# A two-layer decoder kernel: the row-statistics matmuls of the attention contract over 128 rows, 64 of them zeros, instead of 64

## The chip, the core and the metric

The kernel runs on one core of one Trainium2 chip. The metric is device time in microseconds (us), the median of a few runs. The engines named below are TensorE (PE, with its weight loads shown as PEld), VectorE (DVE), ScalarE (ACT), GpSimd (POOL) and the queue of SyncE (SP), which issues most of the transfers (DMA).

## What is computed

Two consecutive layers of a decoder run for a prompt of 1024 tokens and for 32 sample tokens. The change lies in layer 0, in the attention of the prompt: one sliding-window attention A (8 query heads, 2 key heads, head dimension 64) and three dilated groups B of the same shape. The part of the reference that matters:

```python
def banded_attention(q, k, v, span, sink=None):
    # each block of 128 queries reads its own and the previous block of keys
    ...
    s = jnp.einsum('nbqhgd,nbkhd->nbhgqk', qb, kk, preferred_element_type=F32)
    ...
    p, den, lse = _softmax_stats(s, mask, sink_b)
    o = jnp.einsum('nbhgqk,nbkhd->nbqhgd', p, vv.astype(F32))

def _softmax_stats(s, mask, sink):
    s = jnp.where(mask, s, NEG_INF)
    m = s.max(-1)
    if sink is not None:
        m = jnp.maximum(m, sink)
    p = jnp.exp(s - m[..., None])
    den = p.sum(-1)
```

Layer 0 ends with an output projection and a layer norm; layer 1 is a chunkwise mLSTM that begins where layer 0 has ended.

## The kernel before

Operands of the matmuls are kept as a high and a low part (float32r), so that a projection is three matmuls for each 128 rows of the contraction: lines 199 to 201 in `proj_feat`, with 384, 384 and 288 tokens to a chunk. Layer 0 has 2016 of these, the keys' included ("projections" below).

The softmax's maximum of a row is taken ahead, from approximate scores. `stats` multiplies the high parts of the queries (`Qh`, 64 rows of head dimension, loaded by `qh_load`) with the high parts of the keys (rows 0 to 63 of `K1`), one matmul of 256 columns for each head and block of 128 queries (line 437): 256 of them, 8 for each of 32 loaded tiles `Qh`. DVE adds the mask and takes the maximum (line 441). A transpose (line 449) turns the maxima of one key head into rows; they go to DRAM, for B through a minimum over the three groups (`attn_b_max`, lines 564 and 568), and come back as row 65 of the tile `Q2`. Only then do the scores proper run in `scores`: lines 466 and 467 (128 rows of `K1` and `Q1`, then the 65 rows of `K2` and `Q2`) and, for the weighted values, lines 489 to 491. A block of scores is these two and three matmuls; attention A has 30 blocks and B has 70. The tiles `Q1` (512 KB) and `Q2` (260 KB) are loaded once for every two blocks of queries, 24 pairs for B.

`Qh` takes the buffers of `Q1` and `Q2` in turn, so that four of its tiles can be in flight; the scores use the same buffers. All these loads stand in one queue, SP's, in a fixed order with the weight loads (`wr`), and each waits there until its buffer is free.

Streams of work are emitted by `weave` in proportion to their work on PE. The statistics and scores have a priority ahead of the projections, so that the latter fill what the former leave. First the query projections are woven with attention A and with the statistics of groups 1 and 2, then the gate path (`proj_z0`) with the statistics of group 3 and with the scores of B. What is left of B's scores runs with the attention of the sample tokens and the merging of the heads. The order in which the instructions then stand on each engine is fixed when the program is built, and each engine takes its own in that order.

```python
Q1 = self.qh_load(0, kv, hf, ("Q1", "Q2")[hf % 2])
nc.tensor.matmul(st[:, u, :], Q1[:, h, q0:q0 + 128], K1[0:64, w0:w0 + 256], start=True, stop=True)
```

Of the kernel before, what the change touches and what calls it, by code (L numbers as in the profile page):

```python
# [26 lines left out]
def weave(*streams):  # L27
    """emit from several streams in proportion to their work on the tensor engine.
    A stream is (generator, total work); it yields the work that it emitted, or None to let the others go first."""
    live = [[g, 0.0, tot] for g, tot in streams]  # L30
    while live:
        for x in sorted(live, key=lambda x: x[1] / x[2]):
            try:
                w = next(x[0])
            except StopIteration:
                live.remove(x)
                break
            if w is not None:
                x[1] += w
                break  # L40


def ahead(tc, gen, offset):
    """the instructions of a stream, with a priority over what was emitted up to offset instructions before"""
# [14 lines left out]
# PSUM tags that the statistics, and the scores and outputs of the two halves of B, take in turn  # L59
STATS_PS = ("st", "sc")  # L60
AB_PS = ((("sc",), ("av",)), (("sc", "st"), ("av", "tr")), (("sc",), ("av", "pj", "pj")))
# by how many instructions the attention streams go ahead of what is woven with them
AHEAD = (1000, 1000, 60, 300)
# work of woven streams
W1, W2, W3, W4 = (129, 76), (86, 80), (28, 15, 6), (64, 90)
# steps of the second half of B that go with the gate path
EARLY = 9
# every how many blocks of B GpSimd takes the low parts
POOL_LO = 4
# tiles of tokens in the order of the output projections; the sample tokens are tile 8  # L70
ORDER = (0, 1, 2, 3, 4, 5, 6, 8, 7)
# stores on the queue of ScalarE, which makes the data
# [3 lines left out]
class Scratch:  # L76
    """cuts tiles that live together out of two large ones"""
# [20 lines left out]
class Builder:  # L98
# [20 lines left out]
    def wlo(self, out, in_, hi):  # L119
        """as lo, by GpSimd in layer 0"""  # L120
        if not self.layer:
            self.nc.gpsimd.tensor_tensor(out, in_, f(hi), OP.subtract)  # L122
        else:
            self.lo(out, in_, hi)

    def split(self, out, in_, scale=1.0):
        """high and low parts, out[:, 0] and out[:, 1]"""
# [3 lines left out]
    def products(self, ps, x, y, start, stop):  # L131
        """ps (+)= x.T y of operands in high and low parts"""
# [16 lines left out]
    def pair(self, pool, x):  # L149
        """[high | low] parts of the 32 sample tokens side by side"""  # L150
# [5 lines left out]
    def proj_tok(self, ps, i, X, xs, w):  # L156
        """token-major: ps[tokens of tile i, 512 features]; w(k) gives high and low parts of the weights.
        For the sample tokens (i = 8) the products with the low parts of x land in rows 32..63."""
# [13 lines left out]
    def samples(self, xs, x):  # L172
        """the sample tokens of the last chunk in one part"""
# [3 lines left out]
    def proj_sample(self, ps, k, xs, w):  # L177
        """part k of the contraction for the sample tokens, in full float32; four parts take the columns of the
        array side by side, and their products are left in 32 rows each"""
# [4 lines left out]
    def fold(self, out, ps):  # L184
        """the sum of the four parts of the sample tokens' products"""
# [4 lines left out]
    def proj_feat(self, src, X, evac, W=None, chunks=(0, 1, 2)):  # L190
        """feature-major: out[128 features, tokens]; yields after each chunk"""
# [165 lines left out]
    def qh_load(self, g, kv, hf, tag):  # L357
        """high parts"""
        Q = self.qp.tile([64, 4, 256], F32R, tag=tag, name="Qh")
        t = slice(256 * hf, 256 * hf + 256)  # L360
        h = slice(4 * kv, 4 * kv + 4)
        self.store("Qh", f(Q), self.QQ[g].rearrange("(d h) t -> d h t", h=8)[64:128, h, t])
# [37 lines left out]
    def v_load(self, g, kv):  # L400
        """[low | high | 1 1] of each block of keys"""
# [17 lines left out]
    def blocks(self, g, qb):  # L419
        """key blocks of query block qb: (block, kind); kind 0 own, 1 previous"""  # L420
# [3 lines left out]
    def stats(self, g, kv, hf, Q1, K1, ST):  # L424
        nc = self.nc
        for qb in range(2 * hf, 2 * hf + 2):
# [5 lines left out]
            for hp in range(2):  # L432
                st = self.pp.tile([128, 2, 256], F32, tag=STATS_PS[hp], name="st")
                for u in range(2):
                    h = 2 * hp + u
                    q0 = 128 * (qb % 2)
                    nc.tensor.matmul(st[:, u, :], Q1[:, h, q0:q0 + 128], K1[0:64, w0:w0 + 256], start=True, stop=True)  # L437
                for u in range(2):
                    h = 2 * hp + u
                    junk = self.sm.tile([128, 256], F32, tag="junk", name="junk", bufs=3)  # L440
# [4 lines left out]
    def neg_rows(self, ST, dst):  # L445
        """-max, rounded to float32r, as rows (h, qb) of 128 queries, to DRAM"""
# [48 lines left out]
    def od_view(self, OD, g, qb):  # L495
        """places in natural token order of query block qb"""
# [12 lines left out]
    def finish(self, ty, kv, sink_nm=None):  # L509
        """1/denominator rows to DRAM"""  # L510
# [3 lines left out]
        if sink_nm is not None:  # L514
            nm = self.sm.tile([32, 128], F32, tag="nmc", name="nmc")
            self.store('m', nm, sink_nm.rearrange("h (b q) -> (h b) q", q=128))
            e = self.sm.tile([32, 128], F32, tag="snk", name="snk")
            nc.scalar.activation(e, nm, AF.Exp, bias=self.sinkc[:, kv:kv + 1])
            nc.vector.tensor_tensor(dn, dn, e, OP.add)
        rc = self.sm.tile([32, 128], F32, tag="rc", name="rc")  # L520
        nc.vector.reciprocal(rc, dn)
        self.store('m', self.FD[ty][kv].rearrange("h (b q) -> (h b) q", q=128), rc)

    def attn_a(self, kv):
# [3 lines left out]
        for hf in range(4):  # L528
            Q1 = self.qh_load(0, kv, hf, ("Q1", "Q2")[hf % 2])
# [16 lines left out]
    def attn_b_stats(self, g, kv):  # L546
        K1 = self.k1_load(g, kv)
        ST = self.sm.tile([128, 32], F32, tag="ST", name="ST")
        for hf in range(4):
            Q1 = self.qh_load(g, kv, hf, ("Q1", "Q2")[hf % 2])  # L550
# [21 lines left out]
    def attn_b(self, kv, done=None):  # L572
        """the groups into one accumulator; done(c) is called when the tokens of chunk c are complete"""
# [26 lines left out]
    def proj_z0(self, j):  # L600
        nc = self.nc
        sz = self.stage.tile([128, T], F32, tag="sh", name="sz")
        if j < 4:
            kv, c = j // 2, 2 * (j % 2)
            o = self.tmp.tile([128, TP], F32, tag="ao", name="ao")
            F = self.tmp.tile([128, TP], F32, tag="aF", name="aF")
            for u in range(2):
                pr = slice(64 * u, 64 * u + 64)
                self.store('a', o[pr], self.OD[0][kv][0:64, c + u])
                self.store('a', F[pr], self.FD[0][kv][c + u].partition_broadcast(64))  # L610
            nc.gpsimd.tensor_tensor(o, o, F, OP.mult)
# [13 lines left out]
    # Scores have rows (sequence of a half, head, token) and one column per key. The 32 (head, token) queries of  # L625
    # a sequence are stationary, four sequences side by side in the array; the keys of the sequence move.
    def sample_queries(self, sp):
        """queries [128 (kv, d), seq, head, token] of each group, and masked scores of the new keys"""
# [34 lines left out]
    def sample_keys(self, src, g, a, st):  # L663
        """keys or values of the four sequences of half a, as [128, residues, 128] per sequence"""
        out = []
# [11 lines left out]
    def sample_group(self, g, st):  # L677
        """masked scores of the cached keys, and the maximum"""
# [27 lines left out]
    def sample_av(self, g, o, sp, st, first, last):  # L706
        """o[(seq, head, token), half, (kv, d)] += p^T v"""
# [29 lines left out]
    def sample_out(self, o, rec, ty, sp):  # L737
        """normalise, transpose, and place by (head parity, d), head pair, token"""
# [50 lines left out]
    def layer_norm(self, m, r, g, b):  # L789
        """LN(r) * g + b over 1024, in place; all in halves of 512"""  # L790
# [14 lines left out]
    def rstd(self, m, mv, eps, tag, scale=1.0):  # L805
        """(var scale + eps)^-0.5, with a Newton step after the first yield"""
# [12 lines left out]
    def merge0(self, ty, kv, c, M, inverse=True):  # L819
        """normalised attention outputs of four heads times the gate path, tokens of chunk c;  # L820
        the gate path of A has its prompt's outputs in it"""
# [67 lines left out]
    def layer0(self):  # L889
# [3 lines left out]
        # rows (part, d, head): low parts of 64 d, high parts of 64 d, -maximum  # L893
        self.QQ = [dt(f"QQ{g}", [129 * 8, TP]) for g in range(4)]
        self.QS = dt("QS", [4, 512, TS])
        # rows (part, d, head): high parts twice, low parts
        self.KK, self.KS = dt("KK", [3 * 512, TP]), dt("KSd", [512, TS])
        # per (group, kv head): low and high parts of 64 d
        self.VV = dt("VV", [TP, 8 * 128])
        self.NMB = [[dt(f"NMB{i}{g}", [4, TP]) for g in range(3)] for i in range(2)]  # L900
        # numerators of 64 d, denominator
# [12 lines left out]
        with tc.tile_pool(name="qp", bufs=2) as self.qp, tc.tile_pool(name="kp", bufs=2) as self.kp, \  # L914
# [8 lines left out]
            self.load(self.sinkc, A['sinkc'])  # L923
            run(self.proj_q(0))
# [97 lines left out]
    def gates(self):  # L1022
        """per-token gate quantities, in rows [4 heads, tokens]"""
# [596 lines left out]
```

## Time and profile before

| | |
|---|---|
| time, median of 3 runs | 1501.39 us (1501.26 to 1509.19) |
| span of the profiled execution | 1501.1 us |
| PE busy, share of the span | 1429.2 us, 95% |
| DVE busy | 882.7 us, 59% |
| statistics matmuls on PE (line 437) | 256, first at 169.2, last at 463.4 us |
| last projection of layer 0 | about 538 us |
| scores of B end | about 642 us |

The profiled execution's own time is not listed apart from its span; the span lies 0.3 us under the median. Busy time counts an instruction from its first to its last moment. Neighbouring matmuls overlap, so the price of one in a stream is the distance from its start to the start of the next.

### The profile page before, as it was taken

What the parts mean: (1) busy time and instruction counts of PE and PEld (TensorE: products, weight loads), DVE (VectorE), ACT (ScalarE), POOL (GpSimd) and SP (SyncE); (2) the same over time, 40 slices, a digit from 0 to 9 for tenths busy, and PEclk for the clock granted to TensorE, in tenths of its full rate; (3) what the DMA queues carried; (4) which work ended last, traced back from release to release, by engine and by line L of the source; (5) the groups of instructions that cost most, each with busy time, mean ns of one, the idle gap of its engine ahead of it and who ended that gap; (6) DMA issues with size and microseconds to landing.
All of it is one profiled execution on the core that took longest, in us unless ns stands there. A gap on an engine that the chain in (4) does not pass through costs nothing.

```text
span 1501.1 us, 21918 instructions
## 1 busy us (share of the span) xinstructions
PE 1429.2 (95%) x7792; PEld 1186.7 (79%) x7792; DVE 882.7 (59%) x2479; ACT 471.6 (31%) x892; POOL 264.6 (18%) x345
## 2 busy tenths in 40 slices
PE   8999999999999887889999999999999999998997
PEld 8989897977787754457878878988898899877785
DVE  5411455657665676778765536655565566566786
ACT  5331143431112464532123313331333133333310
POOL 1002242422233476501100000100000000000010
PEclk9999999999999997999999999999999999999999
DMA  8646455655766689995412665364323312341731
GB/s 306 224 147 215 161 176 179 206 177 178 198 175 180 187 216 234 273 291 167 156 51 72 202 223 200 96 199 132 77 78 117 117 50 68 116 131 23 249 132 46
DMA packets 148683, 241.01 MB, mean 161 GB/s; under 512 B 17504, under 2 KB 115776, under 8 KB 148056
## 3 DMA queue, kind: packets, MB, share of 16 engines
q1 hardware_dynamic: 140510, 218.24, 48.0%
q10 hardware_dynamic: 8064, 21.37, 4.0%
q8 instruction: 62, 1.02, 0.3%
q14 instruction: 47, 0.39, 0.1%
HBM read 178.66 MB, written 83.97 MB: 175 GB/s over the span
## 4 chain that ended last, share of the span: by engine, by line
PE 47%; DMA 9%; DVE 4%; issue 2%; ACT 1%; SPq 1%; POOL 0%; DVEq 0%; ACTq 0%; POOLq 0%
PE pj L199 5%; PE pj L201 5%; PE pj L200 5%; PE py L165 3%; PE py L167 3%; PE py L166 3%; PE pvo L165 3%; PE pvo L166 3%; PE pvo L167 3%; DMA Q<-QQ 3%; DMA G<-GR 2%; DMA out_cmems_dram<-Cs 1%; DMA wr<-in_wo_dram 1%; DMA mo<-OD 1%; PE S L1232 1%
## 5 line engine op out<-in xcount | busy, mean ns | idle before, releaser
L199 PE MATMUL pj<-xh,wh 128*128 128x384 f32 (+1 forms) x576 | 191.6, 333 | 0.2 <-DVE rt L214 0.2
L199 PE MATMUL pj<-x1h,wh 128*128 128x384 f32 (+1 forms) x576 | 189.6, 329 | 1.7 <-ACT QT L1153 1.6
L201 PE MATMUL pj<-xh,wl 128*128 128x384 f32 (+1 forms) x576 | 190.1, 330 | 0.0
L200 PE MATMUL pj<-xl,wh 128*128 128x384 f32 (+1 forms) x576 | 189.9, 330 | 0.0
L201 PE MATMUL pj<-x1h,wl 128*128 128x384 f32 (+1 forms) x576 | 187.7, 326 | 0.0
L200 PE MATMUL pj<-x1l,wh 128*128 128x384 f32 (+1 forms) x576 | 187.4, 325 | 0.0
L199 PEld LDWEIGHTS pj<-xh,wh 128*128 128x128 f32 x576 | 109.0, 189 | 9.4 <-ACT vv L112 0.8
L201 PEld LDWEIGHTS pj<-xh,wl 128*128 128x128 f32 x576 | 109.2, 190 | 6.0 <-issue 0.2
L200 PEld LDWEIGHTS pj<-xl,wh 128*128 128x128 f32 x576 | 109.2, 190 | 6.0
L199 PEld LDWEIGHTS pj<-x1h,wh 128*128 128x128 f32 x576 | 108.6, 189 | 6.5 <-issue 3.3
L201 PEld LDWEIGHTS pj<-x1h,wl 128*128 128x128 f32 x576 | 108.5, 188 | 6.0 <-issue 5.8
L200 PEld LDWEIGHTS pj<-x1l,wh 128*128 128x128 f32 x576 | 108.6, 189 | 4.0 <-issue 3.8
L441 DVE CUSTOM_DVE_ANT_0 junk<-st,maskq 128x256 f32<-128x256 f32 (+1 forms) x256 | 80.1, 360 | 43.4 <-PE st L437 32.5
L165 PE MATMUL pvo<-voh,x1h 128*128 128x512 f32 x256 | 101.0, 397 | 2.4 <-DVE SZ L1169 2.4
L166 PE MATMUL pvo<-voh,x1l 128*128 128x512 f32 x256 | 100.3, 394 | 0.0
L167 PE MATMUL pvo<-vol,x1h 128*128 128x512 f32 x256 | 99.6, 392 | 0.0
L811 POOL TENSOR_TENSOR rsw<-rsw,mhalf 128x1 f32<-128x1 f32 (+1 forms) x54 | 39.8, 738 | 323.5 <-DVE rsw L810 299.6
L122 POOL TENSOR_TENSOR wl<-wr,wh 128x1024 fp32r<-128x1024 f32 x24 | 57.3, 2389 | 152.4 <-ACT qs L233 102.9
L112 ACT ACTIVATE wh<-wr 128x1024 fp32r<-128x1024 f32 x48 | 50.7, 1056 | 94.5 <-PE pj L200 91.0
L116 DVE TENSOR_TENSOR pl<-p,ph 128x512 fp32r<-128x512 f32 x82 | 66.9, 822 | 21.6 <-ACT ph L112 19.6
L469 ACT ACTIVATE p<-sc 128x512 f32<-128x512 f32 x100 | 57.2, 593 | 59.1 <-PE sc L467 30.8
L112 ACT ACTIVATE ph<-p 128x512 fp32r<-128x512 f32 x100 | 60.7, 627 | 37.0 <-PE av L490 24.8
(348 smaller groups left out, 3109.6 us busy)
## 6 DMA issues: line engine op xcount, KB each, us to landing
Q<-QQ SPq DMA_DIRECT2D x32, 512.0 KB
out_kvs_dram<-in_cache_b_kv_dram SPq DMA_DIRECT2D x16, 1022.0 KB
wr<-in_w0f_dram SPq DMA_DIRECT2D x24, 512.0 KB
wr<-in_w1f_dram SPq DMA_DIRECT2D x24, 512.0 KB
Q<-QQ SPq DMA_DIRECT2D x32, 260.0 KB
QQ<-sh ACTq DMA_DIRECT2D x16, 512.0 KB
QQ<-sl ACTq DMA_DIRECT2D x16, 512.0 KB
Qh<-QQ SPq DMA_DIRECT2D x32, 256.0 KB
```

Of the source, the lines that this page charges most:

```text
L112: return self.nc.scalar.activation(out, in_, AF.Copy, scale=scale)
L116: return self.nc.vector.tensor_tensor(out, in_, f(hi), OP.subtract)
L122: self.nc.gpsimd.tensor_tensor(out, in_, f(hi), OP.subtract)
L165: nc.tensor.matmul(ps, xh[:, k, t], wh, start=k == 0, stop=False)
L166: nc.tensor.matmul(ps, xl[:, k, t], wh, start=False, stop=False)
L167: nc.tensor.matmul(ps, xh[:, k, t], wl, start=False, stop=k == 7)
L199: nc.tensor.matmul(ps[:, :n], wh[:, k, :], xh[:, k, :n], start=k == 0, stop=False)
L200: nc.tensor.matmul(ps[:, :n], wh[:, k, :], xl[:, k, :n], start=False, stop=False)
L201: nc.tensor.matmul(ps[:, :n], wl[:, k, :], xh[:, k, :n], start=False, stop=k == 7)
L441: nc.vector.tensor_tensor_reduce(junk[:, :n], st[:, u, c0:c0 + n], mk, 1.0, -3e38, OP.add, OP.max, ST[:, 8 * h + qb:8 * h + qb + 1])
L469: nc.scalar.activation(p, sc, AF.Exp)
L811: nc.gpsimd.tensor_tensor(r, v, self.mhalf[:m], OP.pow)
```

## The change

`stats` multiplies all 128 rows of `K1` (its rows 64 to 127 repeat the high parts) with a query tile of 128 rows whose rows 64 to 127 are zeros. The zeros are written once, so the query tiles can no longer be buffers that other tiles use: two tiles `QZ` live through the phase and take the loads in turn. Room for them comes from smaller scratch: one buffer `junk` for three, `finish` works in place, and the factor `F` of the gate path is loaded and applied in two halves of 512 tokens. Comments are dropped as well, which the diff here leaves out.

```diff
-    def qh_load(self, g, kv, hf, tag):
-        Q = self.qp.tile([64, 4, 256], F32R, tag=tag, name="Qh")
+    def qh_load(self, g, kv, hf):
+        Q = self.QZ[hf % 2]
         t = slice(256 * hf, 256 * hf + 256)
         h = slice(4 * kv, 4 * kv + 4)
-        self.store("Qh", f(Q), self.QQ[g].rearrange("(d h) t -> d h t", h=8)[64:128, h, t])
+        self.store("Qh", f(Q[0:64]), self.QQ[g].rearrange("(d h) t -> d h t", h=8)[64:128, h, t])
         return Q
...
-                    nc.tensor.matmul(st[:, u, :], Q1[:, h, q0:q0 + 128], K1[0:64, w0:w0 + 256], start=True, stop=True)
+                    nc.tensor.matmul(st[:, u, :], Q1[:, h, q0:q0 + 128], K1[:, w0:w0 + 256], start=True, stop=True)
...
-                    junk = self.sm.tile([128, 256], F32, tag="junk", name="junk", bufs=3)
+                    junk = self.sm.tile([128, 256], F32, tag="junk", name="junk", bufs=1)
...
-            e = self.sm.tile([32, 128], F32, tag="snk", name="snk")
-            nc.scalar.activation(e, nm, AF.Exp, bias=self.sinkc[:, kv:kv + 1])
-            nc.vector.tensor_tensor(dn, dn, e, OP.add)
-        rc = self.sm.tile([32, 128], F32, tag="rc", name="rc")
-        nc.vector.reciprocal(rc, dn)
-        self.store('m', self.FD[ty][kv].rearrange("h (b q) -> (h b) q", q=128), rc)
+            nc.scalar.activation(nm, nm, AF.Exp, bias=self.sinkc[:, kv:kv + 1])
+            nc.vector.tensor_tensor(dn, dn, nm, OP.add)
+        nc.vector.reciprocal(dn, dn)
+        self.store('m', self.FD[ty][kv].rearrange("h (b q) -> (h b) q", q=128), dn)
...
-            Q1 = self.qh_load(0, kv, hf, ("Q1", "Q2")[hf % 2])
+            Q1 = self.qh_load(0, kv, hf)
...
-            F = self.tmp.tile([128, TP], F32, tag="aF", name="aF")
             for u in range(2):
                 pr = slice(64 * u, 64 * u + 64)
                 self.store('a', o[pr], self.OD[0][kv][0:64, c + u])
-                self.store('a', F[pr], self.FD[0][kv][c + u].partition_broadcast(64))
-            nc.gpsimd.tensor_tensor(o, o, F, OP.mult)
+            for t in (slice(0, 512), slice(512, 1024)):
+                F = self.tmp.tile([128, 512], F32, tag="aF", name="aF")
+                for u in range(2):
+                    self.store('a', F[64 * u:64 * u + 64], self.FD[0][kv][c + u, t].partition_broadcast(64))
+                nc.gpsimd.tensor_tensor(o[:, t], o[:, t], F, OP.mult)
...
+            self.QZ = [sm.tile([128, 4, 256], F32R, name=f"QZ{u}") for u in range(2)]
+            for Q in self.QZ:
+                nc.gpsimd.memset(f(Q[64:128]), 0.0)
```

The order of the instructions changes with it. On PE, before, this is where the last statistics matmuls stand (`st`), among projections (`pj`) and ahead of the first scores (`sc`) of group 3; 201 of the 2016 projections stand behind them:

```order
L437 MATMUL st<-K_4017,Qh 128x256 x2
L199 MATMUL pj<-xh_100,wh 128x384
L437 MATMUL st<-K_4017,Qh 128x256 x2
L200 MATMUL pj<-xl_101,wh 128x384
L201 MATMUL pj<-xh_100,wl 128x384
L437 MATMUL st<-K_4017,Qh 128x256 x4
L199 MATMUL pj<-xh_100,wh 128x384
```

They stand close together there, the last four in a row. On PE in the changed kernel the same place, the last statistics matmuls and the first scores, reads:

```order
L437 MATMUL st<-K_3993,QZ_955 128x256 x2
L201 MATMUL pj<-xh_102,wl 128x384
L199 MATMUL pj<-xh_102,wh 128x384
L200 MATMUL pj<-xl_103,wh 128x384
L201 MATMUL pj<-xh_102,wl 128x384
L199 MATMUL pj<-xh_102,wh 128x384
L437 MATMUL st<-K_3993,QZ_955 128x256 x2
L200 MATMUL pj<-xl_103,wh 128x384
L201 MATMUL pj<-xh_102,wl 128x384
L199 MATMUL pj<-xh_104,wh 128x288
L466 MATMUL sc<-Q_4172,K_4159 128x512
L467 MATMUL sc<-Q_4174,K_4163 128x512
```

The statistics now end later among the projections: 98 of 2016 stand behind the last of them. Up to the last projection, 28 matmuls of lines 466 and 467 and 54 of lines 489 to 491 fewer have run than before; they stand behind it.

In SP's queue, before, this is a stretch of the gate path and of the statistics of group 2 (`Qh` from `QQ2`; `aF` and `ao` belong to `proj_z0`, `kt` holds keys, `wr` weights):

```order
L109 DMA Qh_3368<-QQ2_77 64x4x256
L109 DMA Qh_3398<-QQ2_77 64x4x256
L109 DMA aF_4294<-FD00_93 64x1024 x2
L109 DMA ao_4293<-OD00_89 64x1024
L109 DMA Qh_3455<-QQ2_77 64x4x256
L106 DMA kt_4018<-KK_80 128x1024
L109 DMA ao_4293<-OD00_89 64x1024
L109 DMA wr_5068<-in_w0f_dram 128x1024
```

Each `Qh` there is a tile of its own. In SP's queue in the changed kernel, the same stretch:

```order
L109 DMA aF_3818<-FD00_93 64x512 x2
L109 DMA QZ1_955<-QQ2_77 64x4x256
L109 DMA wr_5052<-in_w0f_dram 128x1024
L109 DMA aF_4268<-FD00_93 64x512 x2
L109 DMA ao_4265<-OD00_89 64x1024
L109 DMA QZ0_954<-QQ2_77 64x4x256
L109 DMA ao_4265<-OD00_89 64x1024
L109 DMA QZ1_955<-QQ2_77 64x4x256
L106 DMA kt_3994<-KK_80 128x1024
```

Two tiles alternate where each load had a buffer of its own among four, and the loads of `aF` are twice as many, half as large.

## Rows read from the trace of the kernel before

**Rows 1.** The page's busy times: engine, us (share of span), instructions.
```profile
PE 1429.2 (95%) x7792; PEld 1186.7 (79%) x7792; DVE 882.7 (59%) x2479; ACT 471.6 (31%) x892; POOL 264.6 (18%) x345
```
**Rows 2.** Windows: stretch, length, busy times; last three: clock, DMA share, GB/s.
```profile
160.00:463.40 303.40, 301.82 (x1610) 251.29 (x1609) 181.31 (x647) 83.44 (x148) 89.54 (x64) 0.99 0.61 183
463.40:538.50 75.10, 66.47 (x333) 54.38 (x332) 45.75 (x67) 33.59 (x62) 35.95 (x54) 0.98 0.67 182
538.50:642.00 103.50, 82.69 (x332) 42.21 (x331) 71.88 (x127) 56.95 (x106) 65.05 (x79) 0.85 0.95 252
```
**Rows 3.** Timeline of PE around groups of two and four: start, length, instruction.
```profile
391.19 0.34 PE L199 MATMUL pj<-xh,wh 128*128 128x384 f32 x1
391.37 0.33 PE L200 MATMUL pj<-xl,wh 128*128 128x384 f32 x1
391.63 0.73 PE L437 MATMUL st<-K,Qh 64*128 64x256 f32 x4
...
392.58 0.33 PE L199 MATMUL pj<-xh,wh 128*128 128x384 f32 x1
...
412.52 0.33 PE L200 MATMUL pj<-xl,wh 128*128 128x384 f32 x1
412.69 0.34 PE L201 MATMUL pj<-xh,wl 128*128 128x384 f32 x1
412.96 0.50 PE L437 MATMUL st<-K,Qh 64*128 64x256 f32 x2
413.39 0.44 PE L199 MATMUL pj<-xh,wh 128*128 128x384 f32 x1
413.67 0.34 PE L200 MATMUL pj<-xl,wh 128*128 128x384 f32 x1
```
**Rows 4.** Timeline of PE around two blocks of scores.
```profile
285.76 0.29 PE L201 MATMUL pj<-xh,wl 128*128 128x288 f32 x1
285.89 0.40 PE L466 MATMUL sc<-Q,K 128*128 128x512 f32 x1
286.13 0.39 PE L467 MATMUL sc<-Q,K 65*128 65x512 f32 x1
286.36 0.30 PE L199 MATMUL pj<-xh,wh 128*128 128x288 f32 x1
286.49 0.39 PE L466 MATMUL sc<-Q,K 128*128 128x512 f32 x1
```
**Rows 5.** Groups by line and shape, 160 to 480 us: busy, mean ns, idle before.
```profile
L201 PEld LDWEIGHTS pj<-xh,wl 128*128 128x128 f32 x420 | 79.3, 189 | 5.3 <-issue 0.2
L437 PEld LDWEIGHTS st<-K,Qh 64*128 64x128 f32 x256 | 36.8, 185 | 26.7 <-issue 15.0 <-DVE ST L441 7.3 <-DMA Qh<-QQ 2.0
```
**Rows 6.** Transfers from 538.5 to 642 us, all queues.
```profile
DMA packets 21235, 26.10 MB, mean 252 GB/s; under 512 B 1952, under 2 KB 18602, under 8 KB 21227
```
**Rows 7.** Timelines: loads of Qh, their use, and the pair before one.
```profile
226.84 1.33 SPq L109 DMA_DIRECT2D Qh<-QQ  x2
...
232.19 0.53 PEld L437 LDWEIGHTS st<-K,Qh 64*128 64x128 f32 x4 [0.20 <-DMA Qh<-QQ]
...
422.57 0.50 PE L437 MATMUL st<-K,Qh 64*128 64x256 f32 x2
...
423.10 0.60 SPq L109 DMA_DIRECT2D Qh<-QQ  x1
```
**Rows 8.** SP's own waits, 330 to 463.4 us: total, times, longest.
```profile
SPq L109 <- PE st L437: 32.2, 12, 4.9
```
**Rows 9.** Timeline of PE: transpose of group 3's maxima, first second-half score.
```profile
445.22 0.27 PE L449 MATMUL trm<-ident,ST 128*32 128x128 f32 x1
...
469.70 0.39 PE L467 MATMUL sc<-Q,K 65*128 65x512 f32 x1
```
**Rows 10.** A memset on GpSimd, 160 to 480 us.
```profile
L397 POOL MEMSET K<- 1x1024 f32 x2 | 2.7, 1350 | 3.8 <-PE sc L467 3.7
```
**Rows 11.** A piece of the chain that ended last: start, length.
```profile
554.48 9.27 DMA Q<-QQ
```

More of the change, by code (lines that the diff above doesn't have):

```diff
@@ L549, in attn_b_stats @@
         for hf in range(4):
-            Q1 = self.qh_load(g, kv, hf, ("Q1", "Q2")[hf % 2])
+            Q1 = self.qh_load(g, kv, hf)
             yield from self.stats(g, kv, hf, Q1, K1, ST)
```

## The prediction

> **What bounds the kernel now.** The page's busy times come first [rows 1]: PE is busy for 95% of the span. That is a mean over stages, so the windows come next [rows 2]. From 160 to 463.4 us, where all statistics matmuls run, PE is busy 301.82 of 303.40 us and the DMA share is 0.61: here PE is the bound, and what it saves moves everything behind it. From 463.4 to 538.5 us PE is busy 66.47 of 75.10. In the tail, from 538.5 us, where the projections have run out, to 642 us, where the scores of B end, PE is busy 82.69 of 103.50 while the DMA share is 0.95: the transfers bound it, and work that moves in there costs transfers. Behind 642 us nothing is changed, and I let it follow as it is.
>
> Then the timeline, where distances between starts are to be read [rows 3]. In a stream of projections of 384 columns the starts lie 0.175 us apart (391.19 to 391.37, 412.52 to 412.69). Around a pair of statistics they lie wider: 412.69 to 412.96, 412.96 to 413.39, 413.39 to 413.67, so 0.27, 0.43 and 0.28.
>
> **What a group costs.** From the projection ahead of the pair to the second one behind it is 413.67 - 412.69 = 0.98 us [rows 3]. Two projections are 0.35 of that. A widened statistics matmul of 256 columns should follow the distances of its neighbours: 384 columns take 0.175, 288 columns take 0.13 (285.76 to 285.89, 286.36 to 286.49) [rows 4], so 256 take 0.12. The pair without its gaps would make 0.35 + 0.24 = 0.59, and the gap is 0.39 us. The group of four gives the same: 392.58 - 391.37 = 1.21, less 0.35 and 4 x 0.12 = 0.38 [rows 3]. So the price hangs on a group, not on a matmul. What makes it is the 64 rows and not another operand or shape: the second score, with 65 rows, stands among 128-row matmuls at 0.24 and 0.23, and the projection behind it at 0.13 [rows 4], with no gap. The weight loads say the same. The load for a statistics matmul has 26.7 us of idle time before it, 15.0 of them released by nothing that the profile shows, against 5.3 for 420 projections [rows 5]. With 128 rows in both operands the statistics look like their neighbours.
>
> In the order of before, the 256 statistics stand in 110 groups. 110 x 0.39 = **43 us** off PE. With a widened matmul at the 0.13 of 288 columns it would be 256 x 0.01 less, 40; that is the lower bound, and at 0.11 it would be 46.
>
> One rule would undo this. The Trainium skill (TensorE: Matmul & The Clock Gate, Part 3: Packing small matmuls — row/col tiling, The mechanism) says that a weight load overlaps running matmuls only when it goes to another group of rows. By it the widened statistics, which use the rows of their neighbours, would show their loads, and the sum would lose the 47 us of rival E. The trace does not agree: projections that all load the same 128 rows, at 189 ns a load [rows 5], start 0.175 us apart.
>
> **What moves.** In the changed order the statistics end 103 projections later, and 82 score matmuls (28 and 54) stand behind the last projection that stood ahead of it. At 0.23 each [rows 4] they leave **19 us** before that point. In the tail they cost transfers. 28 score matmuls are 14 of B's 70 blocks, with 24 pairs of Q1 and Q2 for 70 blocks that is 4.8 pairs of 0.77 MB, 3.7 MB, and at the tail's 252 GB/s [rows 6] **15 us**. The bounds: nothing, where they fill PE's idle 21 us of the tail; and the tail's own price of 103.5 us for the 43 blocks that before leaves behind the last projection, 2.4 us each, which for 16 blocks (the mean of 14 blocks by scores and 18 by values) is 39. That tail also holds the sample tokens' attention, so 39 is high; I take 15, since the DMA share says transfers.
>
> **What two tiles cost.** A load into a tile can be issued when the last matmul on the tile's earlier content has run. How long a load takes: issued at 226.84, waited for at 232.19, 5.3 us [rows 7]. How soon SP takes it: a tile's last pair starts at 422.57 and so ends about 422.8, the load that waits for its buffer goes at 423.10, 0.3 us later [rows 7]; in the dense stretch SP waits for a statistics matmul 12 times [rows 8], so it is mostly at the load in time. It needs 5.6 us. What there is: in the changed order, between the last matmul on a tile and the first on its next content stand the other tile's 8 matmuls and 29 to 55 projections; at the distances above that is 5.3 to 9.7 us, 7.8 in the mean, for the 26 loads behind the first six. Four of them have 6.2 or less. So the loads are in time but for a few; with SP late by 1 or 2 us at some of them I take **3 us**, with 0 below. Four buffers, counted in the same way, had some 20 us of room. Behind a QZ load that waits in SP's queue stand weights, keys and the next QZ load, and for these PE waits in the end.
>
> **What waits behind the maxima.** Before, from the transpose of key head 0 of group 3 to the first second-half score is 445.22 to 469.70 = 24.5 us [rows 9]; the chain through DRAM (the store of the maxima, their load, the minimum, its store, the load of Q2) stands between, and I count all of it as needed. In the changed order 98 projections and 34 statistics stand between, 98 x 0.16 (two chunks at 0.175 to one at 0.13) + 34 x 0.12 = 20 us. PE waits for the rest, **4 us** (0 to 5).
>
> **What costs nothing.** Two memsets of 64 x 1024, near 1.35 us each [rows 10], stand on GpSimd ahead of the statistics; GpSimd is busy 18% and nothing but weight splitting queues behind them. The product with F in two halves is the same work in two parts; its second load waits in SP's queue for the first product, and a QZ load stands behind it. What hides this is SP's 32.2 us of waiting for statistics [rows 8]; without that cover each delays a QZ load, which is rival C. One junk buffer is written by one engine in order. DVE is busy 181 of 303 us [rows 2]; with 43 us gone that is 0.70.
>
> **The sum.** -43 - 19 + 15 + 4 + 3 = **-40 us**, from the profiled 1501.1 us (0.3 under the median) to **1461 us**.
>
> **The rivals.**
> - A, the tail takes its full price: 39 for 15. -43 - 19 + 39 + 7 = -16, 1485 us. For it: the chain that ended last goes there through a transfer of Q of 9.3 us [rows 11]. Against: PE is idle there for 21 us.
> - B, the tail absorbs the moved blocks, since fewer weights are loaded beside them: -43 - 19 + 0 + 7 = -55, 1446 us.
> - C, slower: a load of QZ takes longer than its gap. At the 9.3 us that a Q load took in the tail [rows 11], with 0.3 for SP, each of 26 loads is late by 9.6 - 7.8 = 1.8 us, 47 us in all, and the time is 1501 - 40 - 3 + 47 = 1505. It decides from 9.1 us on, where 26 x 1.65 eats the 43 that the rest leaves. Against: the share of the transfers is 0.61 there, not 0.95, and the load seen took 5.3.
> - D, the gap is not the 64 rows' and stays: then only the order moves, -19 + 15 to 39 + 7, 1504 to 1528 us. Against: the 65 rows.
> - E, the weight loads of the widened statistics show: 256 x 0.185 = 47 us back [rows 5], 1508 us. Against: the projections' distances. The Trainium skill's rule on weight loads (TensorE: Matmul & The Clock Gate) would give this.
>
> **How the numbers follow.** Forecast (1450 to 1472) 0.55; A, or loads that are late in part (1472 to 1493), 0.20; B and below 0.09; C 0.05, D 0.03, E 0.03; the rest, between A and no change, 0.05. The predicted time is the forecast's, 1461. The range for 8 in 10 runs from B's side, 1442, to within A, 1489. A measurement tells from no change what is over 0.5%, 7.5 us. Faster by that: 0.55 + 0.20 + 0.09 and a little, 0.85. Same 0.06. Slower 0.09.
>
> **What would show it.** The distance from a projection across a pair to the second behind it falls from 0.98 to about 0.6 us, and line 437 has weight loads without idle time before them. The last statistics matmul starts near 463 - 43 + 17 (its 103 projections) + 3 = 440 us, the last projection near 538 - 43 - 19 + 7 = 483, the scores of B end near 602. PE's idle before line 437 for QZ is a few us; if it is tens of us, C is right and the step on the two tiles failed. If the tail from the last projection is longer than 125 us, the 15 us was too small.

## The result: slower by 0.5%, and the profile after

The changed kernel takes **1512.21 us** (median of 9 runs, 1508.58 to 1515.51), against 1501.39 (1498.45 to 1509.19, 9 runs) for the kernel before on the same chip: ratio 1.0054, 95% interval 1.0036 to 1.0073. The forecast was 1461, range 1442 to 1489. The profiled span is 1512.8 us. Of the runs further down, e3, e5 and e7 each had one execution in a slow state, which their times and ratios leave out.

The page's busy times, to be read beside [rows 1]:

```profile
PE 1409.6 (93%) x7792; PEld 1193.2 (79%) x7792; DVE 897.7 (59%) x2479; ACT 472.9 (31%) x892; POOL 276.4 (18%) x351
```

PE is busy 20 us less than before and the kernel is 12 us longer: the saving is there, and something else costs more. Where, the milestones show. I cut each span at three starts: the last projection of layer 0 (line 201), the last weighted value of the scores (line 491) and the first projection of layer 1 (line 199). They give four stages: **main** (to the last projection), **tail** (to the last weighted value), **exit** (output projection and norm) and **layer 1**. In the kernel before the first two cuts lie at 534.7 and 639.9 us, some 3 us ahead of the rough 538 and 642 that the table and the prediction use.

| us | main | tail | exit | layer 1 | span |
|---|---|---|---|---|---|
| before | 534.7 | 105.2 | 134.2 | 727.0 | 1501.1 |
| after | 494.7 | 145.5 | 142.1 | 730.5 | 1512.8 |
| difference | -40.0 | +40.3 | +7.9 | +3.5 | +11.7 |

All that the main stage wins, the tail loses. (Nothing is changed in layer 1; over the profiled executions of all the kernels here it takes 723.2 to 731.3 us, so its +3.5 is not told from scatter.) The windows of the changed kernel, cut there and at the end of the statistics (columns as in [rows 2]):

```profile
160.00:465.80 305.80, 286.18 (x1717) 269.98 (x1717) 197.80 (x647) 85.97 (x153) 95.12 (x69) 0.98 0.64 190
465.80:494.70 28.90, 24.76 (x131) 21.50 (x130) 13.68 (x29) 9.85 (x19) 16.98 (x27) 0.94 0.81 206
494.70:640.20 145.50, 114.46 (x454) 59.62 (x452) 102.50 (x171) 80.23 (x156) 88.05 (x104) 0.86 0.92 223
640.20:782.30 142.10, 125.92 (x669) 96.44 (x666) 103.14 (x192) 25.39 (x39) 11.49 (x12) 0.95 0.51 155
```

The tail and the exit of the kernel before, cut at the same milestones:

```profile
534.70:639.90 105.20, 85.38 (x344) 43.97 (x342) 73.06 (x125) 58.38 (x110) 67.77 (x83) 0.85 0.94 250
639.90:774.10 134.20, 123.88 (x693) 95.47 (x692) 105.52 (x201) 28.19 (x53) 11.95 (x12) 0.99 0.55 175
```

In the first row of the changed kernel PE is idle for 19.6 us; before it was idle for 1.6 there [rows 2]. The tail is still full of transfers (a DMA share of 0.92, 0.94 before), but holds more of them, at a lower rate. Its transfers, to be read beside [rows 6]:

```profile
DMA packets 27368, 32.39 MB, mean 223 GB/s; under 512 B 2205, under 2 KB 24446, under 8 KB 27358
...
Q<-QQ SPq DMA_DIRECT2D x17, 512.0 KB
Q<-QQ SPq DMA_DIRECT2D x17, 260.0 KB
```

and in the kernel before, cut at the same two milestones, with 13 and 13 loads of `Q`:

```profile
DMA packets 21915, 26.29 MB, mean 250 GB/s; under 512 B 1950, under 2 KB 19316, under 8 KB 21908
```

The gap itself is gone. The timeline of PE around a pair, the counterpart of [rows 3]:

```profile
419.48 0.34 PE L199 MATMUL pj<-xh,wh 128*128 128x384 f32 x1
419.65 0.40 PE L437 MATMUL st<-K,QZ 128*128 128x256 f32 x2
419.89 0.34 PE L200 MATMUL pj<-xl,wh 128*128 128x384 f32 x1
420.07 0.33 PE L201 MATMUL pj<-xh,wl 128*128 128x384 f32 x1
```

From the projection ahead to the second behind it is 420.07 - 419.48 = 0.59 us (0.98 before), and the pair takes 0.24, as forecast. What PE waits for from 160 to 465.8 us instead (total, times, longest):

```profile
PE st L437 <- DVE ST L441: 9.4, 6, 3.5
PE st L437 <- DMA QZ<-QQ: 7.8, 6, 2.4
PE trm L449 <- DVE ST L441: 1.4, 1, 1.4
```

### The profile page after: what moved, and what is told of

Its sections match the earlier page's. It is cut to its first block, busy times and chain, and to the rows that moved or that the text cites. A ratio compares the mean times of both kernels' runs of the same rounds, so it can differ in the third digit from the quotient of the medians.

```text
span 1512.8 us, 21927 instructions
## 1 busy us (share of the span) xinstructions
PE 1409.6 (93%) x7792; PEld 1193.2 (79%) x7792; DVE 897.7 (59%) x2479; ACT 472.9 (31%) x892; POOL 276.4 (18%) x351
## 4 chain that ended last, share of the span: by engine, by line
PE 67%; DMA 18%; DVE 7%; issue 3%; ACT 1%; POOL 1%; SPq 1%; DVEq 0%; POOLq 0%; ACTq 0%
PE pj L199 10%; PE pj L200 10%; PE pj L201 10%; PE py L167 3%; PE py L165 3%; PE py L166 3%; PE pvo L165 3%; PE pvo L166 3%; PE pvo L167 3%; DMA G<-GR 2%; DMA Q<-QQ 2%; DMA NMB<-NM 1%; DMA QZ<-QQ 1%; DMA OD<-OD 1%; PE av L489 1%
## 5 line engine op out<-in xcount | busy, mean ns | idle before, releaser
L199 PE MATMUL pj<-xh,wh 128*128 128x384 f32 (+1 forms) x576 | 187.9, 326 | 1.2 <-DVE rt L214 1.2
L441 DVE CUSTOM_DVE_ANT_0 junk<-st,maskq 128x256 f32<-128x256 f32 (+1 forms) x256 | 93.0, 363 | 25.0 <-PE st L437 5.9
L116 DVE TENSOR_TENSOR pl<-p,ph 128x512 fp32r<-128x512 f32 x82 | 68.3, 842 | 21.7 <-ACT ph L112 15.8
```

The source lines that it names most:

```text
L116: return self.nc.vector.tensor_tensor(out, in_, f(hi), OP.subtract)
L199: nc.tensor.matmul(ps[:, :n], wh[:, k, :], xh[:, k, :n], start=k == 0, stop=False)
L441: nc.vector.tensor_tensor_reduce(junk[:, :n], st[:, u, c0:c0 + n], mk, 1.0, -3e38, OP.add, OP.max, ST[:, 8 * h + qb:8 * h + qb + 1])
```

## The experiments

Theories: **T1**, the widening saves what was forecast, and the scratch that was cut to make room costs it, through the order of the work (transfers of B's scores moved into the tail) and through F's halves. **T2**, the two tiles `QZ` cost it, as loads come late. **T3**, the widening does not save.

All times are medians, each beside the kernel before on the same chip (1501.27 for e1 to e4, 1503.55 for e5 to e8, 1501.52 for e9 to e11); the ratio decides, and stands with its 95% interval. The stages are those of one profiled execution, whose span can lie up to 9 us off the median. "Ahead" counts the matmuls of lines 466 and 467, 200 in all, that the program's order has ahead of the last projection; the fewer, the more are left to the tail.

| | ratio | ahead | main | tail | exit | layer 1 |
|---|---|---|---|---|---|---|
| before | 1 | 114 | 534.7 | 105.2 | 134.2 | 727.0 |
| after | 1.0054 | 86 | 494.7 | 145.5 | 142.1 | 730.5 |
| e1 after, 64 rows | 1.0194 | 86 | 510.3 | 148.7 | 141.7 | 727.5 |
| e3 one junk | 1.0071 | 86 | 519.2 | 135.8 | 130.5 | 723.2 |
| e5 halves | 1.0114 | 104 | 524.3 | 126.7 | 140.0 | 724.4 |
| e6 in place | 1.0006 | 114 | 533.5 | 104.2 | 133.7 | 729.0 |
| e4 all three | 1.0183 | 86 | 514.3 | 140.7 | 141.8 | 728.9 |
| e2 wide, four buffers | 0.9853 | 110 | 503.3 | 115.3 | 128.1 | 731.3 |
| e10 e2, halves | 0.9846 | 112 | 505.2 | 110.4 | 135.9 | 729.8 |
| e9 e2, one junk, in place | 0.9913 | 86 | 491.9 | 132.8 | 131.2 | 727.6 |
| e11 e2, all three | 1.0088 | 86 | 499.4 | 142.3 | 142.1 | 728.2 |
| e7 after, two junk | 0.9931 | 94 | 502.5 | 129.4 | 136.5 | 725.8 |
| e8 wide, low parts | 0.9813 | 110 | 495.2 | 113.5 | 131.7 | 726.0 |

**e1, the changed kernel without the widening.** The order, the tiles and the scratch are those of the changed kernel:

```diff
-  nc.tensor.matmul(st[:, u, :], Q1[:, h, q0:q0 + 128], K1[:, w0:w0 + 256], start=True, stop=True)
+  nc.tensor.matmul(st[:, u, :], Q1[0:64, h, q0:q0 + 128], K1[0:64, w0:w0 + 256], start=True, stop=True)
```

> The changed kernel with one thing undone: the statistics contract over 64 rows again, read from the same two tiles, in the same order of instructions on every engine (118 groups, last statistics matmul ahead of 98 projections). Theory O (the widening saves what was predicted, and the changed order of the instructions gives it back in the tail): the gaps come back, 118 x 0.39 = 46 us on PE, of which the waits of PE for QZ and DVE in the changed kernel (17 us) hide a part; last projection 30 to 46 us later than in the changed kernel, time 1535 to 1558. Rival W (the gap is not the 64 rows'): 1512 as the changed kernel. Rival T (two tiles: loads that are late ate the gain): loads have more time here, the waits for QZ go, 1510 to 1525.

1529.35 us, ratio 1.0194 [1.0148, 1.0240]. T3 falls: in one and the same order the widening saves 1528.2 - 1512.8 = 15.4 us of span, 15.6 of them in the main stage. That is less than the 43 of the forecast, and than the 30 to 46 us that this run was expected to show at the last projection. The window of the statistics says why:

```profile
160.00:481.00 321.00, 320.02 (x1710) 266.25 (x1708) 194.27 (x649) 86.43 (x153) 94.67 (x69) 1.00 0.59 180
```

PE's busy time there falls by 320.02 - 286.18 = 33.8 us, but its idle time grows from 1.0 to 19.6, and the granted clock falls from 1.00 to 0.98. The clock falls behind long waits. After the wait of 3.54 us that ends at 425.50 in the changed kernel, the granted clock from 426 to 428 us is 0.50 (1.2 GHz instead of 2.4), and projections of 384 columns start 0.32 us apart instead of 0.175:

```profile
426.06 0.53 PE L200 MATMUL pj<-xl,wh 128*128 128x384 f32 x1
426.38 0.53 PE L201 MATMUL pj<-xh,wl 128*128 128x384 f32 x1
```

It is 0.50 behind three other waits as well (258.7 to 261, 385 to 387 and 456.7 to 459 us). As an estimate, 0.02 of 305.8 us is 6 us of PE's work: a wait costs more than its length, and without it the 33.8 would be near the 40 of e2 below.

**e2, the widening without the two tiles and without the cuts.** The kernel before, with zeros written into the ordinary four buffers ahead of each load:

```diff
-        Q = self.qp.tile([64, 4, 256], F32R, tag=tag, name="Qh")
+        Q = self.qp.tile([128, 4, 256], F32R, tag=tag, name="Qh")
+        self.nc.gpsimd.memset(f(Q[64:128]), 0.0)
...
-        self.store("Qh", f(Q), ...
+        self.store("Qh", f(Q[0:64]), ...
...
-  ... K1[0:64, w0:w0 + 256], start=True, stop=True)
+  ... K1[:, w0:w0 + 256], start=True, stop=True)
```

> The kernel before, with 128 rows in the statistics: rows 64 to 127 of each of the four alternating query tiles are zeroed by GpSimd before its load. Scratch as before (three junk buffers, F in one piece). 112 groups, 216 projections behind the last statistics matmul, nearly before's order. Theory O: 43 us off PE ahead of the last projection and a tail as before's, so 1455 to 1470. Rival W: 1501. Rival T agrees with O here (four tiles). If the 32 memsets of about 0.95 us on GpSimd delay the weights: up to 10 us of the gain lost.

1478.67 us, ratio 0.9853 [0.9811, 0.9895], slower than the 1455 to 1470 that were expected. The order is nearly that of before (the last statistics matmul at projection 1800, 1815 before), so its first window stands right beside the first of [rows 2]:

```profile
160.00:435.00 275.00, 259.23 (x1596) 244.47 (x1595) 180.06 (x642) 83.63 (x148) 113.50 (x92) 0.99 0.70 202
```

PE busy 301.82 to 259.23 for 14 instructions fewer: 42.6, less some 2 for those, so 40 us. The forecast's 43 (40 to 46) was right as busy time. But PE is idle for 15.8 us (1.6 before), so the statistics end only 28.4 us earlier. What PE waits for from 160 to 435 us:

```profile
PE st L438 <- DVE ST L442: 8.7, 5, 2.6
PE st L438 <- issue: 5.2, 2, 3.5
```

Line 438 is the statistics matmul here, line 442 DVE's maximum: once the gap is gone, DVE's maxima are the next wait.

**e3, e5, e6: the cuts one by one, on the kernel before. e4: all three.** No statistics matmul is widened in them.

```diff
e3, e4
-  junk = self.sm.tile([128, 256], F32, tag="junk", name="junk", bufs=3)
+  junk = self.sm.tile([128, 256], F32, tag="junk", name="junk", bufs=1)
e5, e4
-  nc.gpsimd.tensor_tensor(o, o, F, OP.mult)
+  for t in (slice(0, 512), slice(512, 1024)):
+      F = self.tmp.tile([128, 512], F32, tag="aF", name="aF")
+      ...
+      nc.gpsimd.tensor_tensor(o[:, t], o[:, t], F, OP.mult)
e6, e4
-  nc.vector.reciprocal(rc, dn)
+  nc.vector.reciprocal(dn, dn)
...
```

> The kernel before (64 rows, four query tiles) with only one junk buffer instead of three. The order then has only 97 projections behind the last statistics matmul and 28 + 48 score matmuls fewer ahead of the last projection, as in the changed kernel. Theory O: the last projection comes 10 to 20 us earlier, the tail is 30 to 45 us longer, time 1512 to 1530. Rival T (the tiles are the cause, the scratch is harmless): 1501.

> The kernel before (64 rows, four query tiles, three junk buffers) with F loaded and applied in two halves, nothing else. Its order keeps 198 projections behind the last statistics matmul and has 10 + 15 score matmuls fewer ahead of the last projection. Theory H (the halves cost by themselves, in SP's queue and behind the attention): 1509 to 1518, most of it after the scores of B end. Rival (only the moved scores count): 25 x 0.23 = 6 us earlier at the last projection and some 10 later in the tail, 1503 to 1507.

> The kernel before with finish working in place, nothing else; the order on PE is before's. Theory H: 1501, no difference. Rival (the in-place tiles make the next load of dn wait and cost the time behind the attention): 1506 to 1515.

> The kernel before (64 rows, four query tiles) with all the small edits of the change: one junk buffer, finish in place, F in two halves. Theory O: as with one junk buffer alone and a few us more for the halves, 1515 to 1540. Rival T: 1501 to 1505.

e3: 1510.38 us, 1.0071 [1.0042, 1.0101]. e5: 1520.06, 1.0114 [1.0066, 1.0162]. e6: 1501.57, 1.0006 [0.9971, 1.0041]. e4: 1527.02, 1.0183 [1.0135, 1.0231]. So the in-place finish is free, and the other two are not. e3 ends just under theory O's 1512 to 1530 us, with its last projection and its tail as expected. One junk buffer alone gives the changed kernel's order: the last statistics matmul at projection 1919 (1918 after, 1815 before) and 86 score matmuls ahead of the last projection. Its tail holds 31.19 MB (26.29 before) and is 30.6 us longer. The two tiles had nothing to do with that order. F's halves alone move 10 score matmuls and 15 of the values into the tail, which is 21.5 us longer, and lengthen the exit by 5.8; theory H had expected most of their cost behind the scores, and up to 1518 us. e4 and e1 differ only in the query tiles (four buffers, or two tiles `QZ`), at 64 rows, and agree: 1.0183 and 1.0194.

**e7, the changed kernel with two junk buffers of half the size.** The junk values are written in bfloat16; nothing reads them:

```diff
-  junk = self.sm.tile([128, 256], F32, tag="junk", name="junk", bufs=1)
+  junk = self.sm.tile([128, 256], mybir.dt.bfloat16, tag="junk", name="junk", bufs=2)
```

> The changed kernel (128 rows, two query tiles, F in halves) with two junk buffers of half the width in bytes (bfloat16, in the same room) instead of one. The order has 163 projections behind the last statistics matmul (98 in the changed kernel, 201 before) and 94 and 117 score matmuls ahead of the last projection. Theory O (the one junk buffer moves the scores into the tail): 8 to 18 us faster than the changed kernel, 1494 to 1504. Rival T (two tiles): no change, 1512.

1493.95 us, ratio 0.9931 [0.9902, 0.9961]: 1.2% less than the changed kernel, with the same two tiles. 94 score matmuls stand ahead of the last projection for 86, the last statistics matmul stands 65 projections earlier, and the tail is 16.1 us shorter. The narrower type changed little in DVE's own time (the maxima of 256 columns take 420 ns in the mean, 422 in the changed kernel).

**e8, the widening with data for zeros.** The four ordinary buffers, loaded with all 128 rows; the added rows hold the low parts of the queries, which lie beside the high ones in DRAM. The approximate scores become a little more exact, no zeros are written, and a load has 512 KB for 256:

```diff
-  self.store("Qh", f(Q), self.QQ[g].rearrange("(d h) t -> d h t", h=8)[64:128, h, t])
+  self.store("Qh", f(Q), self.QQ[g].rearrange("(d h) t -> d h t", h=8)[0:128, h, t])
```

> The kernel before with 128 rows in the statistics and no zeros: each of the four alternating query tiles is loaded whole, low and high parts (512 KB for 256), and multiplies all rows of K1. No memset, 8.4 MB more of transfers, order with 216 projections behind the last statistics matmul. Theory O: as the four zeroed tiles, 1465 to 1482; what the transfers cost in the statistics' stretch, where their share is 0.61, is some us. If the transfers bind there: 1485 to 1500.

1475.57 us, ratio 0.9813 [0.9761, 0.9864], the lowest median of the study (its interval overlaps with that of e2). The added 8 MB (32 loads of 256 KB) cost nothing that can be seen: the DMA share from 160 to 433.3 us is 0.75 for 0.61, and PE waits 0.9 us for a load of `Qh`.

**e9 to e11, the cuts on e2.** They ask whether the cuts alone turn e2 into the changed kernel, with no `QZ` tile in it.

```diff
e9: e2 and
-  junk = self.sm.tile([128, 256], F32, tag="junk", name="junk", bufs=3)
+  junk = self.sm.tile([128, 256], F32, tag="junk", name="junk", bufs=1)
... and the in-place finish
e10: e2 and the halves of e5
e11: e2 and all three
```

> The version with zeros filled into the four ordinary buffers (run e2, ratio 0.985), with one junk buffer instead of three and finish in place. In the order the last statistics matmul moves from projection 1800 to 1919 and the scores ahead of the last projection fall from 110 to 86. Theory 1 (the scratch edits cost what they cost alone, on top of any saving): 0.985 x 1.007 = 0.992, about 1490 us; the last statistics matmul about 20 us later than in e2 and the stretch from the last projection to the end of the scores 20 us or more longer. Rival (with the gap gone PE waits for DVE and for loads anyway, so that a later order fills waits that were there): no cost, 0.985, about 1479 us.

> The version of run e2 with the factor F in two halves; nothing else. In the order the last statistics matmul stands at projection 1792 (1800 in e2) and the scores ahead of the last projection are 112 (110), so the order hardly moves. Theory 1 (the halves cost by themselves, through the transfers and waits of GpSimd's product in SP's queue, 1.1 per cent as in e5): 0.985 x 1.011 = 0.996, about 1496 us. Rival (in e5 the halves cost only through the order that they moved): the time of e2, 0.985, about 1479 us.

> The changed kernel but for its two tiles: one junk buffer, finish in place and F in halves as there, and the zeros filled into the four ordinary query buffers before each load. Theory 1 (the scratch edits made the changed kernel slow, the two tiles little): 0.985 x 1.018 = 1.003, about 1506 us, within 0.5 per cent of the changed kernel's 1.0054. Rival (the two tiles were the main cost): 0.99 or less, 1486 us or less.

e9: 1486.71 us, 0.9913 [0.9886, 0.9940]. e10: 1477.88, 0.9846 [0.9801, 0.9892]. e11: 1513.57, 1.0088 [1.0057, 1.0120]. With the cuts and without the tiles the time of the changed kernel is back, to within the intervals: T2 falls and T1 holds, but the sums made by it were 18 us too high for e10 and 8 too low for e11. (e11 has waits that the changed kernel has not: PE's weight loads wait 5.3 us for a fill with zeros. So e11 shows that the loss needs no `QZ` tile, not that these cost nothing.) The halves cost nothing on e2, some 17 us on the kernel before (e5) and some 27 us on e9, so they have no price of their own. On e2 one junk buffer with the in-place finish costs 0.6%, the halves nothing, and all of them 2.4%: most of the loss is in the combination. That the order decides what the halves cost is argued; e9 and e11 both have 86 score matmuls ahead, so that count does not tell it. Of the 28.5 us between the spans of e9 and e11 the main stage has 7.5, the tail 9.5 and the exit 10.9. For the main stage, the waits of DVE from 160 us to the last statistics matmul, in e11:

```profile
DVE sz L622 <- POOL ao L612: 15.0, 4, 6.3
```

In e9 that wait is 4.8 us. DVE stands for GpSimd's product of the halves, its maxima stand behind, and PE behind them. This does not account for the 7.5 us: PE waits for maxima 11.5 us in e11 and 10.4 in e9, and e10, where the halves cost nothing, has 12.3 us of the same wait. One such case in the changed kernel, in time (start, length, idle before):

```profile
421.50 3.35 DVE L621 TENSOR_TENSOR sz<-sz,ao 128x1024 f32<-128x1024 f32 x1 [4.95 <-POOL ao L611]
```
```profile
425.50 0.47 PE L437 MATMUL st<-K,QZ 128*128 128x256 f32 x2 [3.54 <-DVE ST L441]
```

In the tail SP's waits for the second score matmul grow from 17.3 to 27.4 us and the rate falls from 236 to 226 GB/s; no run isolates this. For the exit, the queue of SP tells. The loads of the output projection's weights in e9, in pairs:

```profile
627.54 1.47 SPq L106 DMA_DIRECT2D wr<-in_wo_dram  x2
...
636.75 1.47 SPq L106 DMA_DIRECT2D wr<-in_wo_dram  x2
...
646.44 6.43 SPq L106 DMA_DIRECT2D wr<-in_wo_dram  x2
```

and in the changed kernel, one by one, as in e11, e1, e4 and e5:

```profile
647.94 0.38 SPq L106 DMA_DIRECT2D wr<-in_wo_dram  x1
...
655.60 0.33 SPq L106 DMA_DIRECT2D wr<-in_wo_dram  x1
...
662.90 0.33 SPq L106 DMA_DIRECT2D wr<-in_wo_dram  x1
...
669.96 0.33 SPq L106 DMA_DIRECT2D wr<-in_wo_dram  x1
```

These start 7 to 8 us apart, with other loads and their waits between; for the weights themselves SP waits only 3.0 us from 640.2 to 700 us. ScalarE, which splits these weights, waits for them in the changed kernel from 640.2 to 700 us:

```profile
ACT oh L112 <- DMA wr<-in_wo_dram: 19.7, 5, 4.9
```

before it was 5.8 us from 639.9 to 700, and in e9 4.0 from 624.6 to 690. The five kernels that load one by one have exits of 140.0 to 142.1 us; those with pairs have 128.1 to 135.9, and e7, with one pair, 136.5. The granted clock of the exit falls along with it: 0.92 to 0.95 in the five and in e7, 0.96 to 0.99 in the others. What in the program's construction makes the halves turn pairs into single loads (but not in e10) was not followed up.

## Why the prediction was wrong, step by step

The forecast put the last projection 55 us earlier (-43 - 19 + 7), the tail 15 longer and all behind it unchanged. Measured: 40.0 earlier, 40.3 longer, 11.4 behind. The three errors, 15.0 + 25.3 + 11.4, are the 51.7 us between 1461.1 and 1512.8. The sign that the prediction named for a tail priced too low, over 125 us, came: 145.5. So the step that failed most is the tail's 15 us, which measured 40.3; behind it stands that the cuts were put at nothing, where the changed kernel is 2.0% slower than e2, the same widening without them and without the two tiles.

- **The gap, -43: the price was right, its worth was not.** e2 beside before gives 40 us of PE's busy time, and the pair's distance fell to 0.59. But 14 us of it in e2, and 18.6 of 33.8 in the changed kernel against e1, came back as idle time, with the lower clock on top (e1). The step behind it, that a DVE share of 0.70 costs nothing, failed: the share came out at 0.65 (197.80 of 305.80), but PE waited for maxima 10.8 us. A mean share says little where the work comes in bursts. No run removed DVE's wait, so that it alone is what is left is argued from the waits, not shown.
- **The moved work, -19 + 15: the step that turned the sign.** The shift was read rightly from the order, and the tail paid rival A's full price: 40.3 for 39. Counted as the prediction counts them, 16 blocks cost 2.5 us each, against 2.4 for the 43 that before leaves there, although PE is idle for 31.0 of the 145.5 us; counted by scores on both sides it is 2.9 for 14 blocks, so that 39 came so near is in part luck. The volume of Q was sized rightly (4 pairs more for 4.8), but 6.1 MB more run in the tail, and at 223 instead of 250 GB/s, so bytes over the mean rate were a lower bound. Why the rate is lower stays open: SP waits for the scores (lines 466 and 467) 22.0 us in 14 stays, hardly more than the 20.6 in 6 before; most is added for the sample tokens' scores (line 685: 21.2, from 13.5). In e3, where the shift is made alone, the tail is 30.6 us longer and the main stage 15.5 shorter: the move is worth +15, not -4, up to the end of the tail; exit and layer 1 are 7.5 us shorter in that execution.
- **What costs nothing: this failed twice, and it is the cause.** "One junk buffer is written by one engine in order" is true of the buffer and not of the program, whose order changes with the count of buffers. e3 shows that this cut makes the order that I then costed under "what moves", and e7 that half of it undone makes the changed kernel faster than before. The halves of F were costed as covered by SP's slack; e11 against e9 shows 27 us, over a third of it in the exit, which I had taken as unchanged. The one buffer has a price on DVE too, which was put at nothing. Two maxima that write it start 0.34 us apart (414.80 to 415.14 in the changed kernel), where with three buffers it is 0.22 (415.51 to 415.73 before), and all of them take 13 us more; first before, then the changed kernel:

```profile
L441 DVE CUSTOM_DVE_ANT_0 junk<-st,maskq 128x256 f32<-128x256 f32 (+1 forms) x256 | 80.1, 360 | 43.4 <-PE st L437 32.5 <-PE trm L449 10.4
L441 DVE CUSTOM_DVE_ANT_0 junk<-st,maskq 128x256 f32<-128x256 f32 (+1 forms) x256 | 93.0, 363 | 25.0 <-PE st L437 5.9 <-PE trm L449 5.5 <-DVE ST L441 0.2
```

It is 93.0 to 93.3 us in every run with one buffer and 77.2 to 80.6 in every other. Little of it reaches PE, which waits for maxima 10.4 us in e9 and 8.7 in e2.
- **The two tiles, +3:** PE waits 7.8 us for `QZ`, in six stays, so the term was too small by 5. But e11, with four buffers, is no faster than the changed kernel, and e1 is as fast as e4, so these 5 us are not what decided.
- **The chain behind the maxima, +4:** between the last statistics matmul and the last projection PE is idle for 4.1 us (28.90 - 24.76) in the changed kernel. That it equals the forecast is luck: 2.8 us of it are a wait ahead of line 466, which reads no maxima, only 1.3 us stand ahead of line 467, which does, and before PE was idle there for 8.6 us [rows 2].
- **Rivals.** A's tail came true, with the cuts' other costs on top. B is wrong by 40 us. C: the loads are late by 7.8 us, not by 47. D and E fall with the 0.59 us. On E, the weight loads of the widened statistics, from 160 to 480 us, beside [rows 5]:

```profile
L201 PEld LDWEIGHTS pj<-xh,wl 128*128 128x128 f32 x448 | 85.9, 192 | 1.2
...
L437 PEld LDWEIGHTS st<-K,QZ 128*128 128x128 f32 x256 | 44.7, 196 | 22.6 <-issue 16.5 <-DMA QZ<-QQ 3.5 <-DVE ST L441 1.5
```

They take 196 ns each, and the matmuls of a pair follow at 0.12 us: the loads lie beside the matmuls. The Trainium skill's rule that a load overlaps only with matmuls on other rows (TensorE: Matmul & The Clock Gate, Part 3, The mechanism), taken by itself, is not borne out here. The prediction's second sign, weight loads of line 437 without idle time before them, came as well, though the sum "issue" hardly moved. The number of stays tells (total, times, longest), first before, then the changed kernel:

```profile
PEld st L437 <- issue: 15.0, 63, 0.4
PEld st L437 <- issue: 16.5, 10, 3.8
```

Before, the stays were many and short, at most 0.4 us, as a gap ahead of each group is. They are gone, and in their place stand a few long ones, in which PE waits for maxima or for `QZ`.

## What to carry to other kernels

A change is worth what it saves less what the room for it costs: test the edits that only make room alone, since a scratch buffer's count or a tile's halves can decide where the program puts other work. When the profile shows a stage bound by transfers, price work that moves into it at that stage's own rate for each block, not at bytes over bandwidth (in e3 30.6 us for 4.9 MB more, which the tail's 250 GB/s would put at 20). Here the same saving without the cuts (e2, e8) makes the kernel 1.5 to 1.9% faster, where the change as made is 0.5% slower.

## What the hardware showed that was not expected

- Matmuls over 64 rows among ones over 128 rows cost some 0.36 us of PE for each switch there and back: 40 us over 110 groups, and nothing for a second or fourth matmul in the group [rows 3]. The Trainium skill (TensorEngine Tiling (Array Packing), Key Properties) says that a change of tiling mode drains TensorE; the runs fit that for 64 rows and give it this price, as read from 0.98 against 0.59 us. At 64 columns no gap shows: before, line 490 (128\*64) stands between lines 489 and 491 (128\*66) at the ordinary distances (539.23, 539.46, 539.70).
- A memset of 64 x 1024 on GpSimd ahead of each of 32 loads (e2) cost little that can be seen: 0.95 us each, PE's weight loads waited 2.9 us for them from 160 to 480 us, and POOL is busy for 113.50 us of 275 in the first window (89.54 of 303.4 before).
